# Copying the quadrants of an 8192 x 8192 matrix by whole rows instead of by halves of rows

## The chip, the cores and the metric

The kernel runs on one core of a Trainium2 chip. The metric is the time of one execution on the device in microseconds (us); the median of several runs is compared. The profile is of one further execution, with its own time.

The core has compute engines, which this kernel does not use, and 16 DMA engines, which move bytes from memory to memory. DMAs are issued from queues: the sync queue (SPq in the profile, packets under q1) and the scalar queue (ACTq, packets under q10). One DMA is split over the 16 DMA engines; a packet is one piece that one engine moves, and each engine adds a small completion packet at its end.

## The reference

```python
def setup_inputs():
    return {
        "x": np.random.randn(8192, 8192).astype(np.float32),
    }

def reference(x: np.ndarray) -> np.ndarray:
    return np.fft.ifftshift(x)
```

For even sizes this swaps the quadrants: output row r, left half, is the right half of input row (r + 4096) mod 8192, and output row r, right half, is the left half of that input row. A row has 32 KiB, half a row 16 KiB, the matrix 268.44 MB. Nothing is computed; each byte is read once and written once.

## The kernel before, in words

All copying goes from memory to memory by `copy` (line 28), whose `dma_start` is line 30 of the profile. Its argument `dims` is the access pattern, as pairs of step and count, that both sides share; the source row and column are the shifted ones.

One DMA of the main loop (lines 43 to 48) copies one half of 256 rows: 256 pieces of 16 KiB, one row apart, 4 MiB in all. The slowest dimension, 256, is split over the 16 DMA engines, `per = 16` rows (line 25) to an engine. The loop goes over groups of four blocks of 256 rows, from the bottom of the matrix to the top. In a group the sync queue writes the left halves of the output for blocks 3, 2, 1, 0, and the scalar queue writes the right halves for blocks 1, 0, 3, 2 (line 46), so that the two queues are at work on different blocks.

Ahead of the loop (lines 35 to 41) stand seven small DMAs on the scalar queue. They copy the right halves of the 16 rows that `left_out` (line 47) takes out of one block, as four strips of columns of 4 KiB: the first three strips in two DMAs each, of 14 and 2, 9 and 7, 4 and 12 rows, the last one in a DMA of 16 rows.

Each DMA gets one of eight completion semaphores. A DMA that is to use a semaphore again waits until the earlier DMA with it has landed; the waiting is done by the sequencer that issues, so that later DMAs of the same queue wait behind it. No DMA depends on the data of another.

Of the kernel before, what the change touches and what calls it, by code (L numbers as in the profile page):

```python
# [1 line left out]

# [4 lines left out]


ENGINES = 16


@with_exitstack
def kernel(
    ctx: ExitStack,
    tc: tile.TileContext,
    x: bass.AP,
    out: bass.AP,
):


    nc = tc.nc
    R, C = x.shape
    hr = R // 2
    hc = C // 2
    per = 16
    rows = ENGINES * per

    def copy(queue, row, col, dims):
        src = (row + hr) % R * C + (col + hc) % C
        queue.dma_start(  # L30
            out=bass.AP(out.tensor, out.offset + row * C + col, dims),
            in_=bass.AP(x.tensor, x.offset + src, dims),
        )

    start = R - 3 * rows
    strip = hc // 4
    for n, k in enumerate((14, 9, 4)):
        col = hc + n * strip
        copy(nc.scalar, start + rows - ENGINES, col, [[C, k], [1, strip]])
        copy(nc.scalar, start + rows - ENGINES + k, col, [[C, ENGINES - k], [1, strip]])  # L40
    copy(nc.scalar, start + rows - ENGINES, hc + 3 * strip, [[C, ENGINES], [1, strip]])

    for first in range(R - 4 * rows, -1, -4 * rows):
        for n in (3, 2, 1, 0):
            copy(nc.sync, first + n * rows, 0, [[C, rows], [1, hc]])
            right = first + (n + 2) % 4 * rows
            left_out = ENGINES if right == start else 0
            copy(nc.scalar, right, hc, [[C, rows - left_out], [1, hc]])


# [1 line left out]
_INS = ['x']  # L52
_OUTS = [((8192, 8192), 'float32')]


# [23 lines left out]
```

## Time and profile before

| | us |
|---|---|
| median of 3 runs | 822.09 (822.01 to 822.77) |
| profiled execution | 821.95 |
| its span, first to last instruction | 820.2 |

The profile of such a kernel is read by its DMA lines. The page gives, for 40 equal slices of the span, the share of time in which the DMA engines are busy and the GB/s that they move (bytes copied; each is read and written). Its third part has one row for each queue: packets, MB, and the time that these packets took as a share of the time of 16 engines. Its last part lists the issues by size, with the median time from the issue to the landing. The same figures can be had for any stretch of the span. Chains of waits on the compute engines say nothing here: the only instructions of a compute engine are four initialisations of 0.1 us.

### The profile page before, as it was taken

The page shows a single profiled execution, that of the slowest core. Times are in us where ns is not written, and L with a number is a line of the kernel's source. Part 1 is how long each engine was busy: PE and PEld are TensorE (multiplying, and loading weights), DVE is VectorE, ACT ScalarE, POOL GpSimd, SP SyncE. Part 2 cuts the span into 40 slices and gives each one's busy share as a digit, 9 for nine tenths or more (in the row PEclk, how much of TensorE's full clock was granted, in tenths as well). Part 3 has the DMA queues.
Part 4 walks back from the last instruction along what each step waited for, and adds up shares of the span by engine and source line. Part 5 has one row for each costly group of instructions (what it writes and reads, how often), then busy time and mean ns, then how long its engine had stood idle before and what let it go on. Part 6 is the DMA issues. An engine that isn't in the chain of part 4 may idle for free. (4 is left out here: it accounts for less than half of the span.)

```text
span 820.2 us, 116 instructions
## 1 busy us (share of the span) xinstructions
POOL 0.2 (0%) x4
## 2 busy tenths in 40 slices
POOL 0000000000000000000000000000000000000000
DMA  9999999999999999999999999999999999999998
GB/s 301 329 324 331 331 328 326 327 330 333 335 330 327 332 328 329 332 329 333 324 331 328 322 336 328 332 324 329 328 328 331 327 333 329 328 330 331 325 328 285
DMA packets 17520, 268.44 MB, mean 327 GB/s; under 512 B 1088, under 2 KB 1088, under 8 KB 1152
## 3 DMA queue, kind: packets, MB, share of 16 engines
q1 hardware_dynamic: 8704, 134.22, 51.3%
q10 hardware_dynamic: 8816, 134.22, 47.9%
HBM read 268.44 MB, written 268.44 MB: 655 GB/s over the span
## 5 line engine op out<-in xcount | busy, mean ns | idle before, releaser
L63 POOL MEMSET const-uint8-127<- 128x1 uint8 x1 | 0.1, 103 | 0.0
L63 POOL MEMSET const-bfloat16-1.0<- 128x1 bf16 x1 | 0.1, 102 | 0.0
L63 POOL MEMSET const-float32-0.0<- 128x1 f32 x1 | 0.1, 99 | 0.2 <-issue 0.2
L63 POOL MEMSET const-float32-1.0<- 128x1 f32 x1 | 0.1, 99 | 0.0
## 6 DMA issues: line engine op xcount, KB each, us to landing
out_dram<-in_x_dram SPq DMA_DIRECT2D x32, 4096.0 KB, 101.7
out_dram<-in_x_dram ACTq DMA_DIRECT2D x31, 4096.0 KB, 102.0
out_dram<-in_x_dram ACTq DMA_DIRECT2D x1, 3840.0 KB, 29.3
out_dram<-in_x_dram ACTq DMA_DIRECT2D x1, 64.0 KB
out_dram<-in_x_dram ACTq DMA_DIRECT2D x1, 56.0 KB
out_dram<-in_x_dram ACTq DMA_DIRECT2D x1, 48.0 KB
out_dram<-in_x_dram ACTq DMA_DIRECT2D x1, 36.0 KB
out_dram<-in_x_dram ACTq DMA_DIRECT2D x1, 28.0 KB
```

Of the source, the lines that this page charges most:

```text
L63: nc = _bacc.Bacc("TRN2", target_bir_lowering=False, num_devices=1)
```

## The change

Both queues copy whole rows. A DMA takes 256 rows with both halves, 8 MiB, by a pattern of three dimensions: the row, the half, and the 4096 elements of the half. On the sync queue the output is written left half first (`to`), and the input is read right half first (`back`, with a backward step from half to half). On the scalar queue it is the other way round. The blocks are taken from the top of the matrix down, in groups of four: sync 0, scalar 2, sync 1, scalar 3. Each queue has 16 DMAs. The strips, and with them the shorter DMA, are gone. The slowest dimension is still 256 on both sides.

```diff
-    per = 16
-    rows = ENGINES * per
+    rows = ENGINES * 16
+    blocks = R // rows
 
-    def copy(queue, row, col, dims):
-        src = (row + hr) % R * C + (col + hc) % C
+    def whole_rows(queue, block, right_first):
+        row = block * rows
+        src = (row + hr) % R
+        to = [[C, rows], [hc, 2], [1, hc]]
+        back = [[C, rows], [-hc, 2], [1, hc]]
+        if right_first:
+            dst, dims, of = hc, back, 0
+            dims_of = to
+        else:
+            dst, dims, of = 0, to, hc
+            dims_of = back
         queue.dma_start(
-            out=bass.AP(out.tensor, out.offset + row * C + col, dims),
-            in_=bass.AP(x.tensor, x.offset + src, dims),
+            out=bass.AP(out.tensor, out.offset + row * C + dst, dims),
+            in_=bass.AP(x.tensor, x.offset + src * C + of, dims_of),
         )
 
-    start = R - 3 * rows
-    strip = hc // 4
-    for n, k in enumerate((14, 9, 4)):
-        col = hc + n * strip
-        copy(nc.scalar, start + rows - ENGINES, col, [[C, k], [1, strip]])
-        copy(nc.scalar, start + rows - ENGINES + k, col, [[C, ENGINES - k], [1, strip]])
-    copy(nc.scalar, start + rows - ENGINES, hc + 3 * strip, [[C, ENGINES], [1, strip]])
-
-    for first in range(R - 4 * rows, -1, -4 * rows):
-        for n in (3, 2, 1, 0):
-            copy(nc.sync, first + n * rows, 0, [[C, rows], [1, hc]])
-            right = first + (n + 2) % 4 * rows
-            left_out = ENGINES if right == start else 0
-            copy(nc.scalar, right, hc, [[C, rows - left_out], [1, hc]])
+    for n in range(0, blocks, 4):
+        for a, b in ((0, 2), (1, 3)):
+            whole_rows(nc.sync, n + a, False)
+            whole_rows(nc.scalar, n + b, True)
```

## The prediction

> **What bounds the kernel now.** I read the page first: who is busy, and what the DMA engines do in the 40 slices of the span.
>
> ```profile
> span 820.2 us, 116 instructions
> ...
> POOL 0.2 (0%) x4
> ...
> DMA  9999999999999999999999999999999999999998
> GB/s 301 329 324 331 331 328 326 327 330 333 335 330 327 332 328 329 332 329 333 324 331 328 322 336 328 332 324 329 328 328 331 327 333 329 328 330 331 325 328 285
> DMA packets 17520, 268.44 MB, mean 327 GB/s; under 512 B 1088, under 2 KB 1088, under 8 KB 1152
> ...
> q1 hardware_dynamic: 8704, 134.22, 51.3%
> q10 hardware_dynamic: 8816, 134.22, 47.9%
> HBM read 268.44 MB, written 268.44 MB: 655 GB/s over the span
> ```
>
> No compute engine works. The 16 DMA engines are busy in all slices, and the two queues' packets take 51.3% + 47.9% = 99.2% of 16 engines' span, so nothing waits for an issue. Time is bytes over rate. The packet counts also say how a DMA is laid out: q1 (sync) has 32 DMAs of 256 rows, and 8704 = 32 x (256 + 16), so each row is one 16 KB packet and each DMA adds 16 completions.
>
> Second, the same figures by stage (columns: stretch, its length, POOL, PEclk, DMA share, GB/s):
>
> ```profile
> 0.00:2.00 2.00, 0.20 (x4) 1.00 0.00 0
> ...
> 5.00:17.00 12.00, 0.00 (x0) 1.00 1.01 332
> ...
> 50.00:200.00 150.00, 0.00 (x0) 1.00 1.00 329
> ...
> 803.00:817.00 14.00, 0.00 (x0) 1.00 0.99 325
> 2.00:817.00 815.00, 0.00 (x0) 1.00 1.00 329
> 817.00:818.00 1.00, 0.00 (x0) 1.00 0.48 180
> 818.00:819.00 1.00, 0.00 (x0) 1.00 0.08 33
> 819.00:820.20 1.20, 0.00 (x0) 1.00 0.00 0
> ```
>
> So the profiled execution is 2.0 us without data, 815.0 us at 329 GB/s (268.1 MB), 2.0 us in which the engines run out one after the other, 1.2 us of closing, and 821.95 - 820.2 = 1.75 us outside the span: 821.95 us, 0.14 below the median of 822.09. All but 7 us is the rate.
>
> What does the rate depend on? The stages differ in what is in flight. From 5 to 17 us the sync queue carries left halves of the output nearly alone: a DMA answer for 6 to 18 us gives q1 96.5% of 16 engines' time and the scalar queue, with its strips, 6.8%. From 803 to 817 us the DMA answer has no packet of q1 left: the scalar queue writes right halves alone. Between them both run. 332, 325, and 328 to 331 GB/s: one queue gives what two give, and left or right makes under 1.3% either way.
>
> Third, the issues:
>
> ```profile
> out_dram<-in_x_dram SPq DMA_DIRECT2D x32, 4096.0 KB, 101.7
> out_dram<-in_x_dram ACTq DMA_DIRECT2D x31, 4096.0 KB, 102.0
> out_dram<-in_x_dram ACTq DMA_DIRECT2D x1, 3840.0 KB, 29.3
> ```
>
> A pair of 4 MiB DMAs takes 8.39 MB / 329 GB/s = 25.5 us, and each is 102 us from issue to landing: four of each queue are outstanding. The issue itself has a median of 0.51 us on either queue (the view of line 30). The issue times show one thing more: in the middle the sync queue issues at 598.70 us and the scalar queue at 608.70, so sync runs some 10 us, or 10 / 25.5 x 16 = 6 rows of an engine's 16, ahead. That stagger comes from the strips, behind which the scalar queue issues its first large DMA at 17.3 us; at the end it is why scalar runs alone.
>
> **The change, part by part.**
>
> *Issues.* 71 become 32: 16 on each queue of 512 pieces of 16 KB (8 MiB). Removed are 39 issues of about 0.5 us; they lay beside busy DMA engines, so 0. If an issue with one more dimension took the longest seen, 1.39 us instead of 0.51, it would still be covered: with four DMAs outstanding and 51 us a pair, a freed place leaves about 153 us of work queued, where it was 77. Behind a waiting issue stand only later DMAs of its own queue. Without that cover an issue would cost its 0.5 to 1.4 us, 16 times a queue. I take 0.
>
> *Start.* Both queues issue at 0.73 us; data flows at 2 us as before. That the scalar queue has whole rows at once, and not after the strips, brings nothing, since one queue alone already had 332 GB/s: 0. First issue as slow as the longest: below 1 us.
>
> *Strips.* The seven small DMAs spread one row of 16 KB per engine unevenly. 1088 completions = 64 x 16 + 64, and 14 + 2 + 9 + 7 + 4 + 12 + 16 = 64: a DMA of k rows runs on k engines. If the short ones use a common first k, engines get between 1 and 7 pieces of 4 KB where four would be even. A 16 KB packet takes (99.2% x 16 x 820.2) / 16384 = 0.795 us, so three pieces are 3 x 0.199 = 0.6 us. Without strips the engine that got 1 piece has 0.6 us more to do. If it is the one that ends last, the end moves by +0.6; if the strips favour the wrong engines, by -0.6. The engines' ends lie about 2 us apart now (817 to 819), and cutting the slow one's share is what would hold them together; I take +0.6.
>
> *End.* Both queues now have equal bytes and end together instead of 17 us apart. As 325 GB/s in that stage is 1.2% under 329, this could bring 14 x 1.2% = 0.2 us; the stretch also has engines near their end, so 0.
>
> *Order of addresses.* This is the term that can matter, and the trace does not show it. An engine now takes 16 whole neighbouring rows, both halves in turn (512 KiB contiguous on the output), where each half was taken in another DMA; and the queues, 512 rows apart, start in step instead of 6 rows apart. No row prices this. The nearest are the slices: apart from first and last they lie between 322 and 336 GB/s, which applied to the whole is 815 x 329/322 = 832.7 (+17.7) and 815 x 329/336 = 798.0 (-17.0). I take 0, by the row nearest to it: the rate of the stages did not move with the queue or the half.
>
> Sum: 0 + 0 + 0.6 + 0 + 0 = +0.6 on 821.95, or 822.7 against the median.
>
> **Rivals.**
>
> *Neighbouring halves help (faster).* If finding the second half of a row right behind the first is cheaper for the memory, the rate of the better slices (333) becomes the mean: 815 x 329/333 = 805.2, so 822.09 - 9.8 + 0.6 = 812.9 us. For it: packets of the two queues differ now (51.3% against 47.9% of the same bytes, 0.82 against 0.77 us), so something about order or side has an effect on a packet; the shortest stretches reach 336. Against it: the mean of both stays where it is when one queue works alone.
>
> *The queues in step collide (slower).* Today's 6 rows of stagger vanish with the strips: both queues begin row 0 of their blocks together, at addresses exactly 512 rows (16 MiB) apart but for the half. If streams at such a distance get in each other's way, the low slices (324.5) become the mean: 815 x 329/324.5 = 826.3, so 822.09 + 11.3 + 0.6 = 834.0 us; with 322 it is 840.4. It decides over my forecast from a rate 0.2% lower, 328.3 GB/s, on. For it: nothing in this kernel puts the queues in step again once they are staggered, so the trace has never shown that state. Against it: the 16 engines of one DMA already stand at equal distances (512 KiB) and hold 329. The Trainium skill (DMA: Bandwidth & Descriptors, Latency and other measured facts) reports copies in HBM that lose rate at row pitches of large powers of two (207 GB/s at 512 KiB, 164 at 2 MiB, 103 at 4 MiB) and are whole again with 4 KiB of padding. By its figures a full collision would make the copying an estimated 815 x 207/103 = 1638 us, far more than my price; but the swapped halves set the queues 16 KiB off that distance, which by the same rule is enough, and 512 KiB between the engines stays as it was. No row of this trace shows either.
>
> *It isn't laid out as it says (slower).* If the three-dimensional pattern with its backward step is cut into smaller pieces, the strips give a price: in the DMA answer for 6 to 18 us q10 has 119 packets, of which 55 are strip pieces, in 6.8% of 16 x 12 us = 13.1 us, 0.237 us for 4 KB where a quarter of a large packet is 0.199. The whole copy in 4 KB pieces would be 65536 x 0.237 / 16 = 971 us. Against it: the innermost run is still 4096 floats on both sides.
>
> **How the numbers follow.** A measurement of this kernel can tell about 0.2% (1.6 us) from no change. Rate unchanged: 0.40; as small drifts of the rate count for more than my 0.6 us, of this 0.28 ends within 0.2%, 0.08 slower, 0.04 faster. Neighbouring halves help: 0.25. In step: 0.30. Other layout: 0.05. So faster 0.29, same 0.28, slower 0.08 + 0.30 + 0.05 = 0.43. The likeliest case alone would be 820 to 825. The range reaches into both rivals: 810 leaves out the stronger gains (0.08), 838 the worst slices (0.07) and the other layout (0.05).
>
> **What would show it.** Packets: 16896 in all (2 x 16 x 528), 512 under 8 KB, 134.22 MB a queue; any other count is the third rival. Landing near 204 us with four DMAs of each queue outstanding. My forecast: 328 to 330 GB/s in the long stretches, no stretch with one queue alone, and engines ending over some 3 us. A rate of 333 or of 324.5 through all stages shows the first or second rival. If in-step queues are the cause, a rate that starts low and recovers as they drift apart would show it best. What makes me wrong is the rate: 1 GB/s is 2.5 us, more than all else together.

## The result and the profile after

The changed kernel takes 863.29 us (862.13 to 864.37, 4 runs) against 822.43 us for the kernel before in the same comparison: a ratio of 1.0493 (95% interval 1.0472 to 1.0514). It is slower by 41 us, outside the predicted range of 810 to 838. The profiled execution took 862.71 us with a span of 860.9 us. Here and below a time is the median of all runs, while a ratio leaves out the few runs that are over 1.5% above the fastest of their kernel, so the quotient of two medians can differ from the ratio by up to half a per cent.

The page of the changed kernel, the lines that answer to those of before:

```profile
span 860.9 us, 77 instructions
...
DMA  9999999999999999999999999999999999999999
GB/s 280 315 314 304 308 316 310 314 313 310 311 311 313 308 305 317 310 314 320 306 314 316 315 313 317 312 319 317 316 316 310 321 321 318 311 311 316 316 311 283
DMA packets 16896, 268.44 MB, mean 312 GB/s; under 512 B 512, under 2 KB 512, under 8 KB 512
...
q10 hardware_dynamic: 8448, 134.22, 50.0%
q1 hardware_dynamic: 8448, 134.22, 49.5%
...
out_dram<-in_x_dram SPq DMA_DIRECT2D x16, 8192.0 KB, 195.6
out_dram<-in_x_dram ACTq DMA_DIRECT2D x16, 8192.0 KB, 111.4
```

The packets are the 16896 that whole rows in 16 KB pieces should give, and the DMA engines are again busy throughout (99.5% by the two queues). They do not stand idle; they move the same bytes more slowly. By stages (columns: stretch, its length, POOL, PEclk, DMA share, GB/s):

```profile
2.00:859.00 857.00, 0.00 (x0) 1.00 1.00 313
50.00:200.00 150.00, 0.00 (x0) 1.00 1.00 312
...
350.00:500.00 150.00, 0.00 (x0) 1.00 1.00 314
...
780.00:858.00 78.00, 0.00 (x0) 1.00 1.00 314
859.00:860.90 1.90, 0.00 (x0) 1.00 0.04 17
```

329 GB/s became 313: 815 x 329/313 = 857 us, the whole difference. The last full stage is the telling one. The scalar queue fell behind: its first three DMAs had been issued by 2.4 us, its fourth at 54.85 us and its fifth at 163.12 us, both held back by a completion semaphore that a DMA of the sync queue had used last. From 780 to 858 us the DMA answer has packets of q10 alone (columns: packets, MB, share of 16 engines):

```profile
q10 hardware_dynamic: 1525, 24.46, 100.3%
```

The rate is 314 GB/s there too, so the loss does not need two queues at work.

### The profile page after: what moved, and what is told of

Same layout as the page of the kernel before. It is cut to its first block, busy times and chain, and to the rows that moved or that the text cites. A ratio compares the mean times of both kernels' runs of the same rounds, so it can differ in the third digit from the quotient of the medians.

```text
span 860.9 us, 77 instructions
## 1 busy us (share of the span) xinstructions
POOL 0.2 (0%) x4
## 2 busy tenths in 40 slices
DMA packets 16896, 268.44 MB, mean 312 GB/s; under 512 B 512, under 2 KB 512, under 8 KB 512
## 6 DMA issues: line engine op xcount, KB each, us to landing
out_dram<-in_x_dram SPq DMA_DIRECT2D x16, 8192.0 KB, 195.6
out_dram<-in_x_dram ACTq DMA_DIRECT2D x16, 8192.0 KB, 111.4
```

## The experiments

All ratios are to the kernel before, run beside each kernel on the same chip. It took 821 to 822 us in the comparisons of the first sixteen kernels named here and 811.1 us in that of the last two. The code cuts are shortened: they show the access patterns and row numbers that differ, some of them in words, and not every line.

**The parts of the change: order of blocks, in step, DMA size.** First the halves as before, without the strips.

```diff
-    start = R - 3 * rows
...
-    copy(nc.scalar, start + rows - ENGINES, hc + 3 * strip, [[C, ENGINES], [1, strip]])
...
-            left_out = ENGINES if right == start else 0
-            copy(nc.scalar, right, hc, [[C, rows - left_out], [1, hc]])
+            copy(nc.scalar, first + (n + 2) % 4 * rows, hc, [[C, rows], [1, hc]])
```

> The kernel before without its strips: both queues start in step with whole DMAs of 4 MiB halves. Theory 'adjacency' (an engine that copies the two neighbouring halves of a row one after the other is served worse) and theory 'size' (8 MiB DMAs of 512 pieces are what costs): 822 to 824 us, 329 GB/s, since neither is touched. Rival 'in step' of the prediction (the stagger of the queues was what kept the rate): 830 us or more.

Measured: 823.02 us, ratio 1.0019 (1.0002 to 1.0037). The strips are worth about 0.2%, and their loss is not the 41 us. The queues were then 4.9 us apart in the middle (issues at 614.88 and 619.74 us), against 10 us before, so they are nearer to step but not in it.

Next, both halves of each block on one queue, in the changed kernel's order of blocks, one half a DMA.

```diff
+    for n in range(0, R // rows, 4):
+        for a, b in ((0, 2), (1, 3)):
+            copy(nc.sync, (n + a) * rows, 0, [[C, rows], [1, hc]])
+            copy(nc.scalar, (n + b) * rows, hc, [[C, rows], [1, hc]])
+            copy(nc.sync, (n + a) * rows, hc, [[C, rows], [1, hc]])
+            copy(nc.scalar, (n + b) * rows, 0, [[C, rows], [1, hc]])
```

> Each queue copies both halves of its blocks, as in the changed kernel and in the same order of blocks, but one half a DMA: 4 MiB DMAs, 16 rows of the one half, then 16 of the other. Adjacency, swap and size: 821 to 825 us. If it is the order of blocks (upwards, pairs 0 and 2, 1 and 3) or that one queue has both halves: 860 to 865 us.

Measured: 822.81 us, 1.0021 (1.0002 to 1.0040). Neither the order of blocks nor the sharing of a block's halves by one queue matters.

Then the 8 MiB DMA of three dimensions itself, with the second half of each pair 256 rows away.

```diff
-        to = [[C, rows], [hc, 2], [1, hc]]
-        back = [[C, rows], [-hc, 2], [1, hc]]
+        # jump is 256 or -256 rows; turn is hc for the sync queue, -hc for the scalar queue
+        out dims [[C, rows], [jump * C + turn, 2], [1, hc]]
+        in dims  [[C, rows], [jump * C - turn, 2], [1, hc]]
```

> As the changed kernel (8 MiB DMAs, three dimensions, 512 pieces, left and right in turn, the same blocks in the same order), but the second half of each pair is taken 256 rows on or back, so that two successive pieces are never neighbours. Adjacency: back to 820 to 826 us. Size, or the mere taking of both sides in turn by one queue: stays at 860 to 865 us.

Measured: 825.08 us, 1.0056 (1.0038 to 1.0073). Size, dimensions and halves in turn cost about half a per cent. (This kernel also had fewer DMAs in flight: a median of 103 us from issue to landing, at some 51 us a pair. The backward straight copy below had four of each queue, 205 us, and lost no more.) "Adjacency" seemed to hold. But the straight copies did not fit it:

```diff
-        to, back as above
+        dims = [[C, rows], [hc, 2], [1, hc]]      # both sides (forward)
+        dims = [[C, rows], [-hc, 2], [1, hc]]     # both sides (backward)
```

> Rows copied straight, the halves not swapped (the columns of the output are thus not the reference's), in 16 KB pieces as in the changed kernel, 8 MiB a DMA. Input and output both run forward without a jump. Theory 'swap' (reading a row's halves in the order opposite to the writing is what costs): back to 820 to 826 us. Adjacency and size: stays at 855 to 866 us.

> Rows copied without the swap (columns of the output not the reference's), but right half first on both sides and both queues: input and output both step back inside the row. If a backward step in a row is itself what made the changed kernel slower than the straight copy (833 us): 860 us or more, as here every access has it. If it is the opposite order of reading and writing: 830 to 836, as in the straight copy.

Measured: forward 832.73 us, 1.0147 (1.0132 to 1.0162); backward 825.44 us, 1.0047 (1.0028 to 1.0066). Halves are neighbours on both sides here, and the cost is 1.5% or 0.5%, not 5%.

**One side at a time.** Only the reads, or only the writes, take whole rows; the other side uses the far step.

> As the changed kernel, but the second half of a pair is written 256 rows on or back (so half of the output holds the neighbouring block's rows); the input is read as there, a whole row with its halves in turn. If neighbouring reads are what costs: 855 to 865 us. If neighbouring writes: 821 to 828. If each costs by itself: between, near 843.

> As the changed kernel, but the second half of a pair is read 256 rows on or back (so half of the output holds the neighbouring block's rows); the output is written as there, a whole row with its halves in turn. Neighbouring writes: 855 to 865 us. Neighbouring reads: 821 to 828. Each by itself: near 843.

Measured: 840.48 us, 1.0216 (1.0187 to 1.0245), and 844.58 us, 1.0270 (1.0248 to 1.0292). Together about the whole. I took it at first for "reads cost half and writes half", but the page's queue rows say otherwise. With rows read and writes far:

```profile
q10 hardware_dynamic: 8448, 134.22, 54.8%
q1 hardware_dynamic: 8448, 134.22, 44.6%
```

With rows written and reads far:

```profile
q1 hardware_dynamic: 8448, 134.22, 53.6%
q10 hardware_dynamic: 8448, 134.22, 45.6%
```

The queues have the same bytes, but in the first kernel the packets of the scalar queue (q10) take the longer time, in the second those of the sync queue (q1). Whole rows are on one side of both queues in both kernels. What the slow queue has, and the other has not, is that its whole rows run forward: scalar reads left then right, sync writes left then right. The other queue takes them backward, and its packets take less time, not more.

**Same side, distance, spacing.** A theory in between blamed an engine's write meeting the read of the queue's next piece on the same half.

```diff
-            in_=bass.AP(x.tensor, x.offset + src, dims),                       # halves, swapped
+            in_=bass.AP(x.tensor, x.offset + (row + hr) % R * C + col, dims),  # halves, straight
...
-        src = (row + hr) % R                                      # whole rows
+        src = (row + hr + rows) % R                               # one block on
+        src = (row + hr) % R + (8 if block != 15 else -8)         # 8 rows on
```

> The halves kernel without strips, but each half is read from the same columns that it is written to (halves not swapped; columns of the output not the reference's); no engine takes both halves of a row in turn. New theory 'same side': on an engine the write of one piece runs beside the read of the queue's next piece, and it costs when both are on the same half of neighbouring rows of the same block (input block 4096 rows on). In the changed kernel that holds for every piece, in the kernel before for none, in the two kernels with one side far for every second piece. Here it holds for every piece: 850 to 870 us. If taking the two neighbouring halves in turn is needed for the cost: 821 to 825.

> The changed kernel with the input taken one block of 256 rows further on (the output holds rows moved by 256): halves in turn and swapped on both sides as before, only the distance from reads to writes changes, by 8 MiB. Same side: 822 to 830 us. Halves in turn as such: 860 to 866.

> The changed kernel with the input taken 8 rows (256 KiB) further on, in one block 8 rows back, so that its rows are moved. Tells how near 'near' is: if same side needs neighbouring rows, 822 to 832 us; if the same 512 KiB of an engine, or if it isn't the distance at all, 855 to 866.

Measured: halves straight 822.79 us, 1.0022 (1.0001 to 1.0042); one block on 859.64 us, 1.0469 (1.0454 to 1.0485); 8 rows on 837.63 us, 1.0211 (1.0180 to 1.0241). The first two are against the theory; it fell. The third shows that in the slow form the time does depend on where the rows lie; whether it is the place of the reads against the writes or that of the reads alone, it does not tell.

And the spacing of the engines, 17 rows each, in whole rows and in halves (`rows = ENGINES * 17`):

> The changed kernel with 17 rows to an engine instead of 16 (272 rows a DMA, and 16 rows at the end of each half of the matrix), so that the engines stand 544 KiB apart and not 512. Theory 'alias' (16 engines in step at equal places of stretches a power of two apart get in each other's way, and neighbouring halves keep them closer to equal places): back to 830 us or less. Theory 'adjacency' as an effect within one engine: stays at 858 to 866 us.

> Halves with 17 rows to an engine (272 rows a DMA), swapped as in the reference. If the 544 KiB between engines cost by themselves what whole rows with 17 lost against whole rows with 16 (886 against 863, +2.7%): 844 us. If the spacing matters only together with halves in turn: 822 to 826.

Measured: whole rows 886.21 us, 1.0739 (1.0673 to 1.0804), so worse, not better; halves 822.67 us, 1.0012 (0.9995 to 1.0028). The slow form is sensitive to the spacing; in the halves no effect can be seen. "Alias" by the power of two fell. Of large row pitches the Trainium skill (DMA: Bandwidth & Descriptors, Latency and other measured facts) says that a few KiB of padding give the rate back. Here 32 KiB more between the stretches that the engines were meant to take made the copy slower (1.0739 against 1.0493), so that rule did not help with this one.

**Unlike sides.** The program that goes to the chip names the reason why forward matters. Forward through whole rows, the steps C and hc merge, since 2 x 4096 = 8192; backward they do not. A sync DMA of the changed kernel is, as [step, count] pairs:

```
in  [[8192, 256], [-4096, 2], [1, 4096]]
out [[4096, 512], [1, 1], [1, 4096]]
```

One side has an outermost count of 256, the other of 512. The trace has the same for the output side: it records 512 pieces in one dimension for each sync DMA, 256 x 2 for each scalar DMA. The far copies and the backward straight one have 256 x 2 on both sides, the forward straight one 512 on both, the halves 256 on both. So far only both queues of the changed kernel and of its variants with rows moved or 17 to an engine, and the slow queue of each one-sided copy, have unlike sides. Four kernels part this from forward neighbours. Even and odd rows in separate DMAs (neighbours, sides alike); halves with the input's rows swapped in pairs (no neighbours, sides unlike); and the changed kernel with pieces of 4032 columns, once with a step that cannot merge and once with one that does.

```diff
-        to = [[C, rows], [hc, 2], [1, hc]]
-        back = [[C, rows], [-hc, 2], [1, hc]]
+        to, back = [[2 * C, rows // 2], [hc, 2], [1, hc]], [[2 * C, rows // 2], [-hc, 2], [1, hc]]     # every second row
...
+        out [[2 * C, rows // 2], [C, 2], [1, hc]], in [[2 * C, rows // 2], [-C, 2], [1, hc]]           # halves, unlike
...
+        to, back = [[C, rows], [hc + 64, 2], [1, hc - 64]], [[C, rows], [-hc + 64, 2], [1, hc - 64]]   # gap, like
+        to, back = [[C, rows], [hc, 2], [1, hc - 64]], [[C, rows], [-hc, 2], [1, hc - 64]]             # gap, unlike
```

> Whole rows as in the changed kernel, halves in turn and swapped, but even and odd rows of a block in separate DMAs of 4 MiB, so that rows lie two apart and neither side's steps merge: both sides are 128 x 2 pieces. Theory 'forward neighbours' (one side reads or writes left half and then right half of the same row): 850 to 866 us. Theory 'unlike sides' (one side described as 512 pieces and the other as 256 x 2): 821 to 826.

> The halves kernel without strips, no row's halves in turn, but the input rows of each pair read in swapped order (rows of the output are then swapped in pairs), so that the input side is 128 x 2 pieces and the output side merges to 256. Unlike sides: 850 to 866 us. Forward neighbours: 821 to 826.

> The changed kernel with pieces of 4032 of the 4096 columns of each half (64 columns of each half are not copied, 1.6% fewer bytes), the second piece on the forward side 64 columns further on, so that its steps don't merge and both sides stay 256 x 2. Order, blocks and size of DMAs as in the changed kernel. Unlike sides: near 822 x 0.984 = 809 us. Forward neighbours: near 863 x 0.984 = 849.

> Control for the kernel before: the same pieces of 4032 columns (the same share not copied), but the second piece exactly half a row on, so that the forward side merges to 512 pieces. Both theories: near 849 us. If this too is near 809, the shorter pieces or their 256-byte gap are what changes the rate, and neither kernel says anything of the cause.

| sides | neighbouring halves | us | ratio (95%) |
|---|---|---|---|
| like, every second row | yes | 823.52 | 1.0030 (1.0018 to 1.0041) |
| unlike, halves | no | 854.37 | 1.0404 (1.0383 to 1.0425) |
| like, gap | yes | 822.07 | 0.9998 (0.9966 to 1.0030) |
| unlike, gap | yes | 864.00 | 1.0493 (1.0424 to 1.0562) |

All four go with unlike sides, and the first three against forward neighbours; the fourth, which both theories expected to be slow, shows that the short pieces alone do not give the rate back. The first two move the same bytes in the same number of packets; the page of the one with like sides and then of the one with unlike sides:

```profile
DMA packets 17408, 268.44 MB, mean 327 GB/s; under 512 B 1024, under 2 KB 1024, under 8 KB 1024
```

```profile
DMA packets 17408, 268.44 MB, mean 315 GB/s; under 512 B 1024, under 2 KB 1024, under 8 KB 1024
```

The last two are the same copy but for 256 bytes in the step to the second piece, on each side, and so but for which columns are left out. Both came out slower than expected (809 and 849), so the shorter pieces cost something too; the difference between them, 1.0493 / 0.9998 = 1.050, is that of the change. Again like sides first, then unlike ones:

```profile
GB/s 298 330 323 333 323 330 333 326 331 325 329 319 315 324 331 330 323 325 318 325 330 320 325 327 325 322 329 333 331 325 329 324 332 329 329 329 330 325 324 263
DMA packets 16896, 264.24 MB, mean 324 GB/s; under 512 B 512, under 2 KB 512, under 8 KB 512
```

```profile
GB/s 281 301 318 310 308 307 302 308 301 289 290 294 281 302 325 308 308 323 305 312 304 325 305 302 310 319 311 311 313 312 311 316 313 313 320 313 296 299 301 235
DMA packets 16896, 264.24 MB, mean 305 GB/s; under 512 B 512, under 2 KB 512, under 8 KB 512
```

Same packets, same bytes; leaving out first and last, 31 of the 38 slices of the second are under 315 GB/s, the lowest slice of the first. One thing goes with unlike sides in every run here and was not parted from them: the merged side carries a dimension of count 1 (`[1, 1]` above), which brings it to as many dimensions as the other side.

**Why unlike sides cost.** With unlike sides the time moved with where the rows lie (17 rows, 8 rows on); in halves with like sides 17 rows changed nothing. So perhaps rows are dealt out to the engines in another way then. Two kernels in halves, with like sides, force a dealing by an outermost dimension of 16 (in the first the stretches lie 17 rows apart, since at 16 the steps would merge):

```diff
-            copy(nc.sync, first + n * rows, 0, [[C, rows], [1, hc]])
+            copy(nc.sync, half + n * 272, 0, [[17 * C, 16], [C, 16], [1, hc]])            # blocks
+            copy(nc.sync, first + n * rows, 0, [[C, 16], [16 * C, 16], [1, hc]])          # row by row
```

> Halves, swapped as in the reference, sides alike, an outermost dimension of 16 stretches of 16 neighbouring rows, 17 rows apart (every 17th row follows in four further DMAs): each engine gets one stretch. Theory 'dealing' (like sides are otherwise dealt row by row, and stretches of neighbouring rows for each engine are what costs): 845 to 890 us. If like sides already are dealt in stretches, and unlike sides cost in another way: 821 to 826.

> Halves without strips, sides alike, an outermost dimension of 16 neighbouring rows and in it 16 steps of 16 rows: neighbouring engines get neighbouring rows. Dealing: 821 to 825 us, the same as the halves without it (823). If like sides are otherwise dealt in stretches: no forecast, but another time than that would speak for it.

Measured, on a chip on which the kernel before takes 811.1 us: blocks 835.14 us, 1.0302 (1.0267 to 1.0337); row by row 813.30 us, 1.0032 (1.0013 to 1.0051). As ratios the expected 845 to 890 were 1.028 to 1.083 of 822, so blocks lie at the low end of that, and row by row is as the halves without forcing (1.0019). In stages, blocks first, then row by row:

```profile
50.00:200.00 150.00, 0.00 (x0) 1.00 1.00 324
200.00:350.00 150.00, 0.00 (x0) 1.00 1.00 324
350.00:500.00 150.00, 0.00 (x0) 1.00 1.00 324
```

```profile
50.00:200.00 150.00, 0.00 (x0) 1.00 1.00 333
200.00:350.00 150.00, 0.00 (x0) 1.00 1.00 333
350.00:500.00 150.00, 0.00 (x0) 1.00 1.00 332
```

The pattern meant to give each engine a stretch of neighbouring rows lowers the rate in every stage, 324 against 332 to 333 GB/s, with like sides and no whole rows. That like sides are dealt row by row, and unlike ones in stretches, fits these runs, but no record here names the engine of a packet. It is supported, not shown. Open also: why stretches cost, why 8 rows on cost less and 17 rows more, and the 1.5% of the forward straight copy, whose sides are alike at 512.

## Why the prediction was wrong, point by point

- **What bounds the kernel: right.** Bytes over rate; all 41 us are rate (329 to 313 GB/s).
- **Issues: size wrong, effect right.** I put the longest at 1.39 us. On the sync queue the median is now 45.5 us (the view of line 40 after): it seems to last until room is made for it. It stays covered, as the 99.5% show: the backward straight copy has issues of 42 us and loses 0.5%, the unlike halves have issues of 0.56 us and lose 4%, and the scalar queue alone has the same 314 GB/s after its last issue. That only a queue's own later DMAs stand behind a wait was wrong: the scalar queue waited for semaphores of the sync queue's DMAs.
- **Start, strips, end: right in size, the end not in its course.** The queues did not end together: the scalar queue ran alone from 780 us on, at the same rate. +0.6 us was predicted for the strips; without them the halves lose 0.2% (some 1.6 us, interval 0.2 to 3).
- **Order of addresses: the step that failed.** I wrote "An engine now takes 16 whole neighbouring rows" and took 0 "by the row nearest to it: the rate of the stages did not move with the queue or the half". All stages of before have like sides, so they could not show what unlike ones cost. In place of 0 the term measured some 41 us: the rate fell to 313 GB/s, and the loss goes with unlike sides (1.0404 and 1.0493, against 1.0030 and 0.9998 with like ones). I also put down as a fact of the kernel before that "the 16 engines of one DMA already stand at equal distances (512 KiB)". This came from the 16 in the code; no row showed it, and the forced dealings speak against it. The range came from the same slices (322 to 336 GB/s), and so was too narrow.
- **Rival, neighbouring halves help: wrong.** With like sides they bring nothing (every second row 1.0030, halves without strips 1.0019).
- **Rival, queues in step: right sign, wrong mechanism.** The scalar queue alone ran at 314 GB/s. Nor does the distance of the queues explain unlike halves, which lose 4% at the blocks and pairs of the halves kernel.
- **Rival, not laid out as it says: nearest to it, at 0.05.** I thought of smaller pieces, and the 16896 packets exclude those. It was the description of the two sides that came out other than written, by merging. Of the number of engines the Trainium skill (DMA: Bandwidth & Descriptors, Why a DMA increments its semaphore by 16 and not by 1) says that it follows from the slowest dimension of both sides. 256 and 512 both give 16, and the 512 completions under 8 KB (32 DMAs x 16) agree. What the same dimension does to the rate no row before could tell.
- **Signs: mixed.** Packets as forecast; landing 195.6 and 111.4 us instead of 204, as the scalar queue, waiting for semaphores, had fewer DMAs outstanding; a stage with one queue alone did come, for the same reason.

## What to carry to other kernels

When a copy from memory to memory keeps all engines busy, look at the access patterns as they stand in the built program, not as written: if one side's steps merge and the other's don't, the sides are unlike, and that cost 4 to 5% here at the same packets and bytes (2% to 7% with the rows placed otherwise). A step that can't merge (every second row, or a second piece elsewhere) gave most or all of it back. Like sides are no promise: the forward straight copy still lost 1.5%. An assumption on which engine holds which rows needs a run of its own, since the trace does not say.

## What the runs showed of the hardware that I had not expected

- Two sides with different counts in the outermost dimension lowered the rate: from 329 to 313 GB/s by the change, and from 324 to 305 GB/s over the span between two kernels with the same size and number of packets.
- With DMAs of 512 pieces an issue can take tens of us: a median of 45.5 us on the sync queue of the changed kernel, 42 us on both queues of the backward straight copy, but 0.56 us on the scalar queue of the changed kernel, which had fewer outstanding. With 256 pieces it took 0.51 us.
- One chip ran the kernel before in 811.1 us where the others needed 821 to 822, so absolute times from different chips are not to be compared.
